# Unread products in the waits of four norms, and ten weight tiles held to the heads of a linear attention

## The chip, the cores and the metric

The kernel runs on one core of one Trainium2 chip. The core has a matrix engine (TensorE, PE), a vector engine (VectorE, DVE), a scalar engine (ScalarE, ACT), a general engine (GpSimd, POOL) and a sync engine (SyncE, SP) that issues most of the transfers; each runs its own instructions in order and waits for the others on semaphores. The metric is the time of one execution on the chip, in microseconds (us). TensorE's clock has two levels, 1.2 and 2.4 GHz; the profile gives the clock that was granted as a share of the higher one (PEclk).

## The reference

One sequence of 512 positions of width 1024 goes through a first block (two kinds of attention, then a mixture of experts looked up by keys) and through two hybrid layers. The change is in the layers. Each mixes three branches under gates, projects, normalises and adds, then does the same with a feed-forward part:

```python
def hybrid_layer(x, ...):
    h = rms_norm_2(x, n_pre_mix)
    proj = h @ w_in
    (u_pool, g_q, g_k, g_v, g_r, g_a1, m_cq, m_ckv, m_kr, gate_logits) = jnp.split(proj, IN_OFFSETS, axis=-1)
    y_a = pool_mixer(u_pool, w_pool, pool_scale) @ w_a
    y_b = gla_mixer(g_q, g_k, g_v, g_r, g_a1, w_gla_a2, b_gla_a, gla_norm) @ w_b
    y_c = mla_mixer(m_cq, m_ckv, m_kr, cos, sin, ...) @ w_c
    gates = jax.nn.sigmoid(gate_logits.astype(jnp.float32)).astype(x.dtype).reshape(b, s, N_BRANCH, d)
    merged = gates[:, :, 0] * y_a + gates[:, :, 1] * y_b + gates[:, :, 2] * y_c
    x = x + rms_norm_2(merged @ w_o, n_post_mix)
    h = rms_norm_2(x, n_pre_ffn)
    gu = h @ w_ffn_gu
    ffn = (jax.nn.silu(gu[..., :D_FF]) * gu[..., D_FF:]) @ w_ffn_down
    return x + rms_norm_2(ffn, n_post_ffn)
```

`gla_mixer` is the linear attention: four heads with keys of 64 and values of 128, in eight chunks of 64 positions. Within a chunk it takes masked scores times values, and between chunks a state that decays:

```python
    cum = jnp.cumsum(heads(log_a, GLA_DK), axis=3)
    att = jnp.where(mask, jnp.einsum('bhntd,bhnsd->bhnts', q_dec, k_inv), 0.0)
    o_intra = jnp.einsum('bhnts,bhnse->bhnte', att, vh)
    kv = jnp.einsum('bhnsd,bhnse->bhnde', k_end, vh)
    ...
    o = (o_intra + o_inter).transpose(0, 2, 3, 1, 4).reshape(b, s, GLA_HEADS, GLA_DV)
    o = o * lax.rsqrt(jnp.mean(o * o, axis=-1, keepdims=True) + EPS)
```

## The kernel before, in words

Activations lie with features on partitions: a tensor of width 1024 is eight tiles of 128 x 512. Every projection goes through `lin`: for each output tile of 128 features and each tile of the input it issues three wide products (`mm3`, L186 to L188), since weights and inputs are split into a high and a low part: high weight by high input, high by low, low by high. A load of weights (`WS.load`, L83 to L102) brings a tile `wr` of 128 x 1024 by SP, ACT casts it to `wh` (L99) and another engine subtracts to get `wl` (L100); there are three buffers of each. A tile serves eight steps, so 24 wide products. Output tiles land in PSUM, are evacuated by a function given to `lin`, and then free their buffer.

In a layer's mix the order is: the input projections, the latent attention, the linear attention `gla`, the gate projection `wgate` (24 output tiles of 24 products), the c projection `wc` and the b projection `wb` (eight output tiles of 12 products each, four weight tiles each), then `wo`. The gate products depend only on the normalised input (`hn`), and the c products only on the latent attention (`yc`), so a scheduler may put them between the small steps of the linear attention. It is a list scheduler that simulates the engines and picks what it thinks is ready, engine by engine; the chip then runs each engine's list in order. `keep_in_program_order` pins an instruction in its engine's order, `issue_after` holds one until a named instruction has been put in. In `load`, the list `hold` says after which instruction the casts of the next weight tiles may go; a held tile's subtraction is on POOL instead of DVE. Before, only the norms fill that list (`self.hold = sq + [self.norm_ins] * 2`, for the three tiles after a norm).

In `gla` the two halves `d` cover heads 0 and 1, then 2 and 3. In each, PE makes the cumulative sums `pc`, `pl` (L718, L719), transposes `tp` (L735) and the chunk states `kv` (L744); ACT copies `kt` (L737); DVE builds the states `st` (L752, L754). For each head PE makes the scores `at` (L762), DVE masks them into `am` (L764), PE makes the output `o` (L768, L774), ACT squares it into `osq` (L776), and PE sums the columns into `pss` (L252). At the end come the norm's broadcast `bc` (L270) and the split into `ybh`, `ybl`.

The gate's evacuation (L607) ends in a store of a tile `sig`. The c evacuation `evc` (L621 to L626) loads that tile into `gc` (two buffers, shared with the gate's `sg`), combines it with PSUM on DVE (L624), adds on POOL (L625) and stores `m` (L626). The b evacuation (L638, L639) has six buffers.

After `wo` and after the ffn's down projection, `post_norm` takes the squares' column sum `pss`, then `rstd_small` (ACT root L260, DVE reciprocal L263), a broadcast `bc` by PE, and per tile DVE's L363 and L364; the next projection starts once ACT has written `hnh` (L316) and DVE `hnl` (L320). There are four such norms: after `wo` and after the ffn in each of two layers.

Of the kernel before, what the change touches and what calls it, by code (L numbers as in the profile page):

```python
# [14 lines left out]
AF = mybir.ActivationFunctionType  # L15
# [5 lines left out]
P = 128  # L21
S = 512
D = 1024
KD = D // P
NT = S // P
# [53 lines left out]
class WS:  # L79
# [7 lines left out]
    def load(self, p):  # L87
        if p not in self.have and p < self.ap.shape[0]:
            nc, wp = self.b.nc, self.b.wp
            raw = wp.tile([P, PW], F32, tag="wr", name="wr", bufs=3)  # L90
            nc.sync.dma_start(raw, self.ap[p])
            hi = wp.tile([P, PW], F32R, tag="wh", name="wh", bufs=3)
            lo = wp.tile([P, PW], F32R, tag="wl", name="wl", bufs=3)
            eng = self.eng
            with ExitStack() as es:
                if self.b.hold:
                    es.enter_context(self.b.tc.issue_after(self.b.hold.pop(0)))
                    eng = nc.gpsimd
                nc.scalar.copy(hi, raw)  # L99
                eng.tensor_tensor(lo, raw, hi.bitcast(F32), OP.subtract)  # L100
            self.have[p] = (hi, lo)
# [14 lines left out]
class Builder:  # L116
# [155 lines left out]
                                  start=True, stop=True)  # L272
        return bc

    def rstd_row(self, parts, dim, sp, hp=None, tok=None, by=1.0):

        p = self.ps(name="pss")
        self.colsum(p, 0, parts, pin=hp is not None)
        r2 = self.rstd_small(p, NT, dim, sp, by)
        bc = self.bcast(r2, 0)  # L280
        if hp is None:
            return bc
        t = hp.tile([P, S], F32, tag="bcs", name="bcs")
        self.nc.any.tensor_copy(t, bc)
        if tok is None:
            return t
        r4 = hp.tile([P, NT], F32, tag=tok, name=tok)
        self.nc.vector.tensor_copy(r4, r2[:, 0:NT])
        return t, r4
# [44 lines left out]
    def post_norm(self, ws, nk, xs, g, side):  # L334

        nc = self.nc
        es = ExitStack()
        sp = self.pool(es, "post", side=side)
        f = sp.tile([P, KD, S], F32, tag="f", name="f")
        parts, sq = [], []  # L340

        def ev(c, p):
            i = self.sq_part(sp, parts, p, c == KD - 1)
            if c == KD - 1:
                sq.append(i.ins)
            if c == KD - 2:
                self.preload(parts[0][:, 0:1])
            if c % 2:
                nc.vector.tensor_scalar(f[:, c], p, g[:, c:c + 1], None, OP.mult)
            else:  # L350
                nc.scalar.activation(f[:, c], p, AF.Copy, scale=g[:, c:c + 1])
        self.lin(ws, nk, KD, xs, ev)
        bc = self.rstd_row(parts, D, sp)
        self.hold = sq + [self.norm_ins] * 2
        old, new = self.xd, self.new_x()

        def get(k):
            self.xd = old
            x = self.x_tile(sp, k, KD if self.final is not None else 5)
            self.xd = new  # L360
            eng = nc.gpsimd if self.final is not None and k in (0, 2, 4) else nc.vector
            pin = self.tc.keep_in_program_order
            pin(nc.vector.tensor_tensor(f[:, k], f[:, k], bc, OP.mult))  # L363
            i = eng.tensor_tensor(x, x, f[:, k], OP.add)  # L364
            if eng is nc.vector:
                pin(i)
            if self.final is not None:
                nc.sync.dma_start(self.final[:, k], x)
            else:
                nc.sync.dma_start(new[k], x)  # L370
            return x
        return get, es
# [124 lines left out]
    def layer_mix(self, l, vb, a, hn, acc, hp, sig_d, ya_d, er):  # L497
        nc = self.nc
        v = self.vecs
        bc = r4 = None  # L500
# [6 lines left out]
        gq = gi.tile([P, 2, S], F32, name="gq")  # L507
        gk = gi.tile([P, 2, S], F32, name="gk")
        gv = gi.tile([P, NT, S], F32, name="gv")
        gr = gi.tile([P, 4, S], F32, name="gr")  # L510
        kr = gi.tile([P, S], F32, name="kr")
# [4 lines left out]
        with ExitStack() as e2:  # L516
            sp = self.pool(e2, "tmpA")
# [48 lines left out]
        with ExitStack() as e2:  # L566
            sp = self.pool(e2, "tmpB")
# [19 lines left out]
        ybh = yp.tile([P, 4, S], F32R, name="ybh")  # L587
        ybl = yp.tile([P, 4, S], F32R, name="ybl")
        gt = self.pool(er, "gates", side="right")
        with ExitStack() as e2:  # L590
            sp = self.pool(e2, "mla")
            for i in range(4):
                o = self.ps("a", name="o")
                self.causal_pair(sp, [([(qT[0:96, h], kT[0:96, h])],
                                       lambda b, h=h: vt[:, b, h * 64:(h + 1) * 64], None)
# [2 lines left out]
        em.close()  # L598
        with ExitStack() as e2:
            gp = self.pool(e2, "gla")  # L600
            self.gla(l, gp, gq, gk, gv, gr, kr[0:32], vb, ybh, ybl)
        eg.close()


        def evg(c, p):
# [6 lines left out]
                nc.vector.scalar_tensor_tensor(t, t, 1.0, y, OP.add, OP.mult)  # L612
            nc.sync.dma_start(sig_d[c], t)
        self.lin_tags = "b"
        self.lin(WS(self, a("wgate")), KD, 24, hn, evg)
        self.lin_tags = "bc"
        m_d = [self.dp.tile([P, S], F32, tag=f"m{i}", name=f"m{i}", bufs=2) for i in range(KD)]
# [75 lines left out]
    def gla(self, l, gp, gq, gk, gv, gr, a1, vb, yh, yl):  # L693
        nc = self.nc
# [13 lines left out]
            nc.vector.scalar_tensor_tensor(la[:, 2 * h:2 * h + 2], z, 0.0, ab, OP.min, OP.subtract)  # L708
        umat, lmat, mask = self.tri[:, 0:P], self.tri[:, P:2 * P], self.tri[:, 2 * P:3 * P]
        oall = gp.tile([P, 4, S], F32, name="oall")  # L710
        pss = self.ps(name="pss")
        for d in range(2):
            ds = slice(d * P, (d + 1) * P)
# [42 lines left out]
            for hh in range(2):  # L756
                h = 2 * d + hh
                r = slice(hh * 64, hh * 64 + 64)
                at = self.ps(shape=[P, NT, P], name="at")
                for b in range(NT):  # L760
                    bs = slice(b * P, (b + 1) * P)
                    nc.tensor.matmul(at[:, b], ki[r, bs], qd[r, bs], start=True, stop=True)  # L762
                am = gp.tile([P, NT, P], F32, tag="am", name="am", bufs=2)
                nc.vector.tensor_tensor(am, at, mask.unsqueeze(1).to_broadcast([P, NT, P]), OP.mult)  # L764
                o = self.ps(name="o")
                for b in range(NT):
                    bs = slice(b * P, (b + 1) * P)
                    nc.tensor.matmul(o[:, bs], gv[:, b, h * P:(h + 1) * P], am[:, b], start=True, stop=False)  # L768
                    for j in range(2):
                        n = 2 * b + j  # L770
                        if n == 0:
                            continue
                        cs = slice(n * 64, n * 64 + 64)
                        nc.tensor.matmul(o[:, cs], st[r, n], qd[r, cs], start=False, stop=j == 1)  # L774
                osq = gp.tile([P, S], F32, tag="osq", name="osq", bufs=2)
                nc.scalar.activation(osq, o, AF.Square)  # L776
                self.colsum(pss, h, [osq])
                nc.any.tensor_copy(oall[:, h], o)
        r2 = self.rstd_small(pss, 16, 128, gp)
        for h in range(4):  # L780
            t = gp.tile([P, S], F32, tag="yt", name="yt", bufs=2)
            bc = self.bcast(r2, h)
            nc.vector.scalar_tensor_tensor(t, oall[:, h], v[:, vb + 36 + h:vb + 37 + h], bc, OP.mult, OP.mult)
            nc.vector.tensor_tensor(t, t, gr[:, h], OP.mult)
            self.split(yh[:, h], yl[:, h], t)

# [1012 lines left out]
```

## Time and profile before

| what | value |
|---|---|
| median of 3 runs | 3681.76 us (3679.64 to 3682.37) |
| the profiled execution | 3670.07 us, its span 3668.3 us |
| mean granted clock of PE | 0.978 |
| busy PE / DVE / ACT / POOL | 3497.4 / 2303.4 / 1397.4 / 1111.2 us |
| busy share of PE | 95% |

The span is one profiled execution on the slowest core; a busy time is the sum over that engine's instructions, and busy PE is not PE at its peak. In the trace the mix of layer 0 ends, with the column sum of its norm, at about 2388 us, the ffn of layer 0 at 2761, the mix of layer 1 at 3279 and the last ffn at about 3651. The linear attention of layer 0 is at about 2204 to 2318.

### The profile page before, as it was taken

What the parts mean: (1) busy time and instruction counts of PE and PEld (TensorE: products, weight loads), DVE (VectorE), ACT (ScalarE), POOL (GpSimd) and SP (SyncE); (2) the same over time, 40 slices, a digit from 0 to 9 for tenths busy, and PEclk for the clock granted to TensorE, in tenths of its full rate; (3) what the DMA queues carried; (4) which work ended last, traced back from release to release, by engine and by line L of the source; (5) the groups of instructions that cost most, each with busy time, mean ns of one, the idle gap of its engine ahead of it and who ended that gap; (6) DMA issues with size and microseconds to landing.
All of it is one profiled execution on the core that took longest, in us unless ns stands there. A gap on an engine that the chain in (4) does not pass through costs nothing.

```text
span 3668.3 us, 46596 instructions
## 1 busy us (share of the span) xinstructions
PE 3497.4 (95%) x17784; PEld 2968.8 (81%) x17784; DVE 2303.4 (63%) x3583; ACT 1397.4 (38%) x2159; POOL 1111.2 (30%) x637
## 2 busy tenths in 40 slices
PE   9979999999999899999999999999999999999998
PEld 7856668998999799888888768878887867778886
DVE  5354454999999699999975544554326363464433
ACT  5534433434665233323333443342223344233221
POOL 1002101666667786666620000231101000131100
PEclk9979999999999999999999999999999999999999
DMA  3212143565888999999952323433333333443332
GB/s 129 96 39 92 55 155 100 185 200 194 295 294 296 328 332 352 351 339 348 340 204 88 131 98 127 158 124 97 109 96 112 115 105 103 158 144 103 96 120 75
DMA packets 229016, 631.25 MB, mean 172 GB/s; under 512 B 22644, under 2 KB 57144, under 8 KB 228792
## 3 DMA queue, kind: packets, MB, share of 16 engines
q1 hardware_dynamic: 191928, 494.04, 39.9%
q0 software_dynamic: 36864, 134.23, 10.2%
q8 instruction: 139, 2.28, 0.3%
q14 instruction: 85, 0.70, 0.1%
HBM read 542.20 MB, written 85.98 MB: 171 GB/s over the span
## 4 chain that ended last, share of the span: by engine, by line
PE 71%; DVE 19%; issue 4%; DMA 2%; ACT 2%; POOL 1%; SPq 1%; ACTq 0%; DVEq 0%; POOLq 0%
PE ps L186 17%; PE ps L188 17%; PE ps L187 17%; PE v L186 3%; PE v L187 3%; PE v L188 3%; DVE og L1561 3%; PE o L415 2%; DVE nr L1411 2%; DVE e L1555 2%; PE s L392 2%; DMA wr<-in_pv 1%; PE tp L409 1%; DVE av L1425 1%; ACT wh L99 1%
## 5 line engine op out<-in xcount | busy, mean ns | idle before, releaser
L99 ACT CAST wh<-wr 128x1024 fp32r<-128x1024 f32 x599 | 626.6, 1050 | 1097.7 <-PE ps L187 741.2
L186 PE MATMUL ps<-hnh,wh 128*128 128x512 f32 (+1 forms) x2616 | 979.7, 378 | 16.2 <-ACT hnh L316 11.3
L188 PE MATMUL ps<-hnh,wl 128*128 128x512 f32 (+1 forms) x2616 | 978.4, 374 | 16.1 <-POOL wl L100 16.1
L187 PE MATMUL ps<-hnl,wh 128*128 128x512 f32 (+1 forms) x2616 | 976.7, 373 | 0.1
L100 POOL TENSOR_TENSOR wl<-wr,wh 128x1024 fp32r<-128x1024 f32 x215 | 562.5, 2618 | 699.7 <-ACT wh L99 592.4
L100 DVE TENSOR_TENSOR wl<-wr,wh 128x1024 fp32r<-128x1024 f32 x384 | 478.3, 1246 | 400.1 <-ACT wh L99 387.2
L186 PEld LDWEIGHTS ps<-hnh,wh 128*128 128x128 f32 x2616 | 498.1, 191 | 85.6 <-ACT hnh L316 12.2
L188 PEld LDWEIGHTS ps<-hnh,wl 128*128 128x128 f32 x2616 | 495.9, 190 | 87.5 <-POOL wl L100 19.6
L187 PEld LDWEIGHTS ps<-hnl,wh 128*128 128x128 f32 x2616 | 496.4, 190 | 67.0 <-DVE hnl L320 2.0
L186 PE MATMUL v<-ah,wh 128*128 128x384 f32 x1024 | 349.8, 342 | 44.9 <-ACT wh L99 44.7
L187 PE MATMUL v<-al,wh 128*128 128x384 f32 x1024 | 345.4, 338 | 0.0
L186 PEld LDWEIGHTS v<-ah,wh 128*128 128x128 f32 x1024 | 193.1, 189 | 57.2 <-ACT wh L99 56.4
L188 PE MATMUL v<-ah,wl 128*128 128x384 f32 x1024 | 228.3, 336 | 0.0
L1411 DVE SCALAR_TENSOR_TENSOR nr<-nr,xt 128x1024 f32<-128x1024 f32 x128 | 210.3, 1658 | 13.5 <-DMA nr<-in_ur,gx 13.5
L1425 DVE SCALAR_TENSOR_TENSOR av<-nr,na,av 128x1024 f32<-128x1024 f32 x127 | 211.4, 1665 | 1.6
L187 PEld LDWEIGHTS v<-al,wh 128*128 128x128 f32 x1024 | 193.3, 189 | 0.0
L675 POOL TENSOR_TENSOR sg<-sg,bcs 128x512 f32<-128x512 f32 x44 | 75.7, 1720 | 374.2 <-ACT sg L674 373.9
L1399 POOL DMA_INDIRECT nr<-in_ur,gx x128 | 176.0, 1375 | 39.7 <-issue 13.1
L188 PEld LDWEIGHTS v<-ah,wl 128*128 128x128 f32 x1024 | 182.9, 188 | 0.9 <-POOL wl L100 0.6
L625 POOL TENSOR_TENSOR gc<-gc,gy 128x512 f32<-128x512 f32 x16 | 24.2, 1513 | 522.6 <-DMA wr<-in_wb 237.8
L223 ACT CAST ah<-at 128x384 fp32r<-128x384 f32 x112 | 57.1, 512 | 328.0 <-DVE at L1334 224.6
L1399 POOL DMA_INDIRECT nr<-in_vr,gx x128 | 161.1, 1259 | 40.3 <-issue 19.0
(490 smaller groups left out, 5534.4 us busy)
## 6 DMA issues: line engine op xcount, KB each, us to landing
wr<-in_pu SPq DMA_DIRECT2D x128, 512.0 KB
wr<-in_pv SPq DMA_DIRECT2D x125, 512.0 KB
wr<-in_wgu SPq DMA_DIRECT2D x88, 512.0 KB
g_d<-gs SPq DMA_DIRECT2D x64, 384.0 KB
gt<-g_d SPq DMA_DIRECT2D x32, 768.0 KB
wr<-in_wgate SPq DMA_DIRECT2D x48, 512.0 KB
wr<-in_wdn SPq DMA_DIRECT2D x44, 512.0 KB
a_d<-ga SPq DMA_DIRECT2D x56, 384.0 KB
```

Of the source, the lines that this page charges most:

```text
L99: nc.scalar.copy(hi, raw)
L100: eng.tensor_tensor(lo, raw, hi.bitcast(F32), OP.subtract)
L186: self.pe(nc.tensor.matmul(out, w[0], x[0], start=start, stop=False))
L187: self.pe(nc.tensor.matmul(out, w[0], x[1], start=False, stop=False))
L188: self.pe(nc.tensor.matmul(out, w[1], x[0], start=False, stop=stop))
L392: nc.tensor.matmul(s[:, 0:n], q[:, t * P:n], k[:, 0:n], start=i == 0, stop=False)
L415: nc.tensor.matmul(o[j * 64:j * 64 + 64, b * P:S], heads[j][1](b), pts[j], start=first and b == 0, stop=last and b == NT - 1)
L675: nc.gpsimd.tensor_tensor(t, t, bc, OP.mult)
L1399: i = nc.gpsimd.indirect_dma_start(out=w[:], out_offset=None, in_=self.a[src], in_offset=bass.IndirectOffsetOnAxis(ap=self.near_i[:, j:j + ...
L1411: nc.vector.scalar_tensor_tensor(u, u, 1.0, xts[group[j]], OP.mult, OP.mult, accum_out=a[:, j:j + 1])
L1425: nc.vector.scalar_tensor_tensor(av, w, a[:, j:j + 1], av, OP.mult, OP.add)
L1561: nc.vector.tensor_tensor(o, e1, two(gT[:, i, tt]), OP.mult)
```

## The change

Two things are added. `keep_awake(n)` issues n products of a 128 x 128 bf16 identity with itself, broadcast to 512 columns, into a PSUM tile `idle` that nothing reads. `rstd_row` takes `warm=(3, 13)` from `post_norm`: three such products between the column sum and the broadcast, thirteen behind the broadcast, all pinned, and the column sum pinned too. That is 64 products in the program.

Secondly `gla` hands out the squares of heads 1, 2 and 3, and the list `hold` gets 28 entries before the gate projection: 18 that hold nothing (the tile is cast whenever it is ready, and subtracted on DVE), then three gate tiles after head 1's square, three after head 2's, and after head 3's the four weight tiles of the c projection.

```diff
-                if self.b.hold:
-                    es.enter_context(self.b.tc.issue_after(self.b.hold.pop(0)))
+                h = self.b.hold.pop(0) if self.b.hold else None
+                if h is not None:
+                    es.enter_context(self.b.tc.issue_after(h))
                     eng = nc.gpsimd
...
+    def keep_awake(self, n):
+
+        p = self.ps(shape=[P, NT, P], name="idle")
+        wide = self.identb.unsqueeze(1).to_broadcast([P, NT, P])
+        for _ in range(n):
+            self.tc.keep_in_program_order(self.nc.tensor.matmul(p, self.identb, wide, start=True, stop=True))
+
-    def rstd_row(self, parts, dim, sp, hp=None, tok=None, by=1.0):
+    def rstd_row(self, parts, dim, sp, hp=None, tok=None, by=1.0, warm=None):
 
         p = self.ps(name="pss")
-        self.colsum(p, 0, parts, pin=hp is not None)
+        self.colsum(p, 0, parts, pin=hp is not None or warm is not None)
+        if warm:
+            self.keep_awake(warm[0])
         r2 = self.rstd_small(p, NT, dim, sp, by)
         bc = self.bcast(r2, 0)
+        if warm:
+            self.keep_awake(warm[1])
...
-        bc = self.rstd_row(parts, D, sp)
+        bc = self.rstd_row(parts, D, sp, warm=(3, 13))
...
-            self.gla(l, gp, gq, gk, gv, gr, kr[0:32], vb, ybh, ybl)
+            late = self.gla(l, gp, gq, gk, gv, gr, kr[0:32], vb, ybh, ybl)
...
+        self.hold = [None] * 18 + [late[i] for i in (0, 0, 0, 1, 1, 1, 2, 2, 2, 2)]
         self.lin(WS(self, a("wgate")), KD, 24, hn, evg)
...
-                nc.scalar.activation(osq, o, AF.Square)
+                late.append(nc.scalar.activation(osq, o, AF.Square).ins)
...
+        return late[1:]
```

PE's list of layer 0 in the first half of the linear attention, before, from the last gate products ahead of head 0's column sum (`ps<-hnh,wh` and its like are gate products):

```order
L187 MATMUL ps<-hnl,wh 128x512
L188 MATMUL ps<-hnh,wl 128x512
L252 MATMUL pss<-ones,osq 128x1 x4
L762 MATMUL at<-qd,ki 128x128 x4
L186 MATMUL ps<-hnh,wh 128x512
L187 MATMUL ps<-hnl,wh 128x512
```

And of the change, from the two gate products behind the transposes to the second head's output (its line numbers are larger by 1 to 14):

```order
L188 MATMUL ps<-hnl,wh 128x512
L189 MATMUL ps<-hnh,wl 128x512
L758 MATMUL kv<-gv,kt 128x256 x7
L776 MATMUL at<-qd,ki 128x128 x4
L782 MATMUL o<-am,gv 128x128
L788 MATMUL o<-qd,st 128x64
...
L788 MATMUL o<-qd,st 128x64 x2
L253 MATMUL pss<-ones,osq 128x1 x4
L776 MATMUL at<-qd,ki 128x128 x4
L782 MATMUL o<-am,gv 128x128
```

Before, 22 gate products stand between head 0's output and its column sum and 23 behind the next scores; from the transposes to head 1's column sum there are 118 in all. Of the change, two are left, and the others stand behind head 1's column sum.

DVE's list at the c projection of layer 0, before (`gc<-gc,ps` is an evacuation of the c projection, `wl<-wr,wh` the subtraction of a weight tile, `am` and `st` belong to heads 2 and 3):

```order
L754 SCALAR_TENSOR_TENSOR st<-st,e_19110,kv 64x128 x2
L624 SCALAR_TENSOR_TENSOR gc<-gc,ps 128x512
L100 TENSOR_TENSOR wl<-wr,wh 128x1024
L754 SCALAR_TENSOR_TENSOR st<-st,e_19110,kv 64x128 x2
L764 TENSOR_TENSOR am<-at,c_tri 128x512
L754 SCALAR_TENSOR_TENSOR st<-st,e_19110,kv 64x128 x2
L624 SCALAR_TENSOR_TENSOR gc<-gc,ps 128x512
L100 TENSOR_TENSOR wl<-wr,wh 128x1024
L624 SCALAR_TENSOR_TENSOR gc<-gc,ps 128x512
L764 TENSOR_TENSOR am<-at,c_tri 128x512
```

And of the change:

```order
L798 TENSOR_TENSOR yt<-yt,gr 128x512
L225 TENSOR_TENSOR ybl<-yt,ybh 128x512 x2
L619 TENSOR_TENSOR sg<-ps,bcs 128x512
L637 SCALAR_TENSOR_TENSOR gc<-gc,ps 128x512 x2
L101 TENSOR_TENSOR wl<-wr,wh 128x1024 x2
L637 SCALAR_TENSOR_TENSOR gc<-gc,ps 128x512 x3
L101 TENSOR_TENSOR wl<-wr,wh 128x1024
L637 SCALAR_TENSOR_TENSOR gc<-gc,ps 128x512
L651 SCALAR_TENSOR_TENSOR gt<-gt,ps 128x512 x2
L228 SCALAR_TENSOR_TENSOR ml<-gt,mh 128x512
```

The evacuations stood among the steps of the linear attention; now they follow it, and the third c evacuation has the subtractions of the first two b tiles ahead of it.

SP's list at the same place, before (`sig` are the stored gate tiles, `m` the stored result of an evacuation, `wr` a load of weights):

```order
L621 DMA gc<-sig_17053 128x512
L626 DMA m_20117<-gc 128x512
L623 DMA gy<-sig_17038 128x512
L621 DMA gc<-sig_17054 128x512
L91 DMA wr<-in_wb 128x1024
L626 DMA m_20118<-gc 128x512
L623 DMA gy<-sig_17039 128x512
L621 DMA gc<-sig_17055 128x512
L626 DMA m_20119<-gc 128x512
```

And of the change:

```order
L91 DMA wr<-in_wb 128x1024
L634 DMA gc<-sig_17054 128x512
L650 DMA gy<-m_20117 128x512
L91 DMA wr<-in_wb 128x1024
L639 DMA m_20118<-gc 128x512
L636 DMA gy<-sig_17039 128x512
L91 DMA wr<-in_wo 128x1024
L634 DMA gc<-sig_17055 128x512
L639 DMA m_20119<-gc 128x512
```

The loads of the last b tiles and the first `wo` tile moved ahead of the c evacuation's third and fourth loads of `gc`.

## Rows read from the trace of the kernel before

**Rows 1.** The page, the chain that ended last by engine.
```profile
PE 71%; DVE 19%; issue 4%; DMA 2%; ACT 2%; POOL 1%; SPq 1%; ACTq 0%; DVEq 0%; POOLq 0%
```

**Rows 2.** Windows: from:to, length, busy (count) per engine, PEclk, DMA share, GB/s.
```profile
2222.00:2237.00 15.00, 15.00 (x76) 11.60 (x75) 9.08 (x19) 3.75 (x5) 0.00 (x0) 1.00 0.30 103
2260.50:2264.00 3.50, 3.50 (x17) 3.38 (x18) 0.00 (x0) 1.18 (x2) 0.00 (x0) 0.53 0.00 0
2301.60:2308.20 6.60, 6.60 (x20) 5.24 (x20) 1.82 (x2) 2.47 (x3) 1.89 (x1) 0.51 0.48 159
222.00:233.00 11.00, 7.97 (x52) 5.46 (x50) 3.67 (x12) 6.26 (x28) 0.00 (x0) 1.00 0.01 1
```

**Rows 3.** Timeline of PE, linear attention: start, length, engine, line, operation [idle before].
```profile
2226.05 0.39 PE L187 MATMUL ps<-hnl,wh 128*128 128x512 f32 x1
2226.28 0.40 PE L188 MATMUL ps<-hnh,wl 128*128 128x512 f32 x1
...
2227.78 1.99 PE L744 MATMUL kv<-gv,kt 64*128 64x256 f32 x14
...
2240.93 0.38 PE L768 MATMUL o<-am,gv 128*128 128x128 f32 x2
...
2244.03 0.66 PE L774 MATMUL o<-qd,st 64*128 64x64 f32 x4
...
2250.74 1.16 PE L762 MATMUL at<-qd,ki 64*128 64x128 f32 x8
...
2261.21 0.79 PE L718 MATMUL pc<-c_tri,la 128*128 128x128 f32 x2
...
2266.59 0.95 PE L252 MATMUL pss<-ones,osq 128*128 128x1 f32 x8
...
2303.62 1.11 PE L774 MATMUL o<-qd,st 64*128 64x64 f32 x4
```

**Rows 4.** Timelines of ACT and DVE, same stretch.
```profile
2222.74 0.59 ACT L737 COPY kt<-tp 128x512 f32<-128x512 f32 x1 [3.01 <-PE tp L735]
...
2229.59 3.37 DVE L754 SCALAR_TENSOR_TENSOR st<-st,e,kv 64x128 f32<-64x128 f32 x9
```

**Rows 5.** Timeline of PE, start of the b projection.
```profile
2319.36 1.20 PE L186 MATMUL ps<-ybh,wh 128*128 128x512 f32 x4 [2.21 <-ACT ybh L223]
```

**Rows 6.** Timelines of DVE, POOL, SP and ACT: c evacuation, weight tiles.
```profile
2295.35 0.69 DVE L624 SCALAR_TENSOR_TENSOR gc<-gc,ps 128x512 f32<-128x512 f32 x1 [3.12 <-DMA gc<-sig]
...
2306.15 1.22 DVE L100 TENSOR_TENSOR wl<-wr,wh 128x1024 fp32r<-128x1024 f32 x1
...
2281.90 1.29 POOL L625 TENSOR_TENSOR gc<-gc,gy 128x512 f32<-128x512 f32 x1 [237.82 <-DMA wr<-in_wb]
...
2387.30 7.42 POOL L100 TENSOR_TENSOR wl<-wr,wh 128x1024 fp32r<-128x1024 f32 x3 [39.15 <-ACT wh L99]
...
2288.26 0.32 SPq L626 DMA_DIRECT2D m<-gc  x1
...
2292.25 0.32 SPq L621 DMA_DIRECT2D gc<-sig  x1
...
2313.20 1.04 ACT L99 CAST wh<-wr 128x1024 fp32r<-128x1024 f32 x1 [0.30 <-DVE rs L263]
```

**Rows 7.** Timelines of PE and DVE: an identity product, norms and their successors.
```profile
183.81 0.39 PE L1138 MATMUL so<-mkb,identb 128*128 128x512 bf16 x1
...
2393.31 2.92 PE L186 MATMUL ps<-hnh,wh 128*128 128x512 f32 x6 [3.46 <-ACT hnh L316]
...
2395.19 0.74 DVE L320 SCALAR_TENSOR_TENSOR hnl<-xk,c_vecs,hnh 128x512 fp32r<-128x512 f32 x1
...
2771.07 0.63 PE L187 MATMUL ps<-hnl,wh 128*128 128x512 f32 x1
2771.50 0.63 PE L188 MATMUL ps<-hnh,wl 128*128 128x512 f32 x1
...
2413.33 0.38 PE L252 MATMUL pss<-ones,sqa 128*128 128x1 f32 x2 [1.27 <-POOL sqa L246]
```

More of the change, by code (lines that the diff above doesn't have):

```diff
@@ L710, in gla @@
         oall = gp.tile([P, 4, S], F32, name="oall")
+        late = []
         pss = self.ps(name="pss")
```

## The prediction

> **What bounds the kernel now.** I read the chain of waits first: TensorE (PE) carries 71% of it [rows 1], so time moves only where PE stands still or runs at its lower clock. Then I cut the linear attention of layer 0 into windows. In a window with gate products between its small steps PE is busy without a gap at granted clock 1.00, yet in two short ones, right behind a block of small products, the clock is 0.53 and 0.51 while PE stays busy [rows 2]. Then PE's timeline: a wide product starts 0.23 us after the one before, so a weight tile (24 of them) is 5.6 us and one output tile of the c or b projection (12) is 2.8 us; the attention's own steps follow with their durations [rows 3]. What they wait for is in the timelines of VectorE (DVE) and ScalarE [rows 4]. The b projection starts after a gap of 2.21 us [rows 5]. Last the path by which the c projection leaves PSUM [rows 6], and the norm after a projection [rows 7]. Layer 1 repeats layer 0, so what follows is for one layer and taken twice, the norms apart.
>
> **First half of the linear attention (heads 0 and 1).** Before, some 118 gate products stand between the transposes and the second column sum; afterwards two. The products are not lost, they come later, but the waits they covered now show. The steps alone take before: kv 1.99, two score blocks of 1.16, an output block 3.76 (2240.93 to 2244.69) and another like it, cumulative sums 3.4 (2261.21 on, at the lower clock), two column sums of 0.95 [rows 3]: 17.2, less 0.1 at each seam, where the next starts before the last ends: 16.5 us.
> Afterwards, from the end of the transposes (t = 0): the copy of kt takes 0.59, so kv runs from 0.6 to 2.6. DVE's state updates start 1.8 behind kv's start (2227.78 to 2229.59) and take 3.37/9 = 0.37 each [rows 3, 4]. The scores need the PSUM buffer that the fourth update frees: 4.0 to 5.1. Their masking stands on DVE behind ten updates, to 6.2, and takes 0.7 (the 128x512 operation of rows 6): the output block can start at 6.9. PE has been busy for 3.6 of 6.9 us.
> At full clock the rest is: output block to 10.7, its square 0.6 and column sum 0.95 to 12.2, scores to 13.4, masking 0.7, output block to 17.9, cumulative sums at half of 3.4 to 19.6, column sum to 20.5. That is 4.0 more than before.
> But a dense mix already fell to 0.53 after one output block [rows 2]; here two and all their waits follow each other with nothing dense between. I let the clock fall before the first output block. At the lower clock four products of that block take 1.11 against 0.66 [rows 3], so the block takes 6.4: to 13.3; square and column sum (0.6 and 1.4) to 15.3, scores (1.9) to 17.2, masking to 17.9, output block to 24.3, cumulative sums 3.4 to 27.7, column sum 1.4 to 29.1. The first gate products behind it start 0.43 apart instead of 0.23 [rows 7]; five of them lose 1.0: 30.1. Against 16.5 this is **+13.6** per layer; bounds +4.0 (clock stays) and +16 (the clock returns later). Against the fall speaks one row: 11 us in which PE was busy for only 8 at clock 1.00 [rows 2].
> The Trainium skill (TensorE: Matmul & The Clock Gate, What's actually happening) says that the clock is set by how busy PE has lately been and that idleness costs half of it. By that rule the fall comes; the trace agrees in two windows and not in the one just named, and no run here shows an attention without cover.
>
> **Second half.** Heads 2 and 3 keep seven and two wide products between their blocks; before, it had more, and still fell to 0.51 for 6.6 us [rows 2]. Two output blocks stand nearly together now: I take **+1.5**, bounds -3.2 (the dip of 6.6 us at half speed goes) and +5.
>
> **Held weight tiles.** The subtraction of a held tile moves to GpSimd, 7.42/3 = 2.5 instead of 1.22 [rows 6]. Behind head 1's square a cast (1.05) and this need 3.6; the cumulative sums and column sum (4.8 at the lower clock) cover them. At full clock 1 us would show. PE then takes 5.6 per tile against 2.5, so nothing else waits. **0**, bounds 0 and +1.5.
>
> **Gap before the b projection.** It goes, since gate and all c products now stand behind the broadcast: **-2.2** [rows 5].
>
> **The c projection without breaks.** Before, its eight output tiles are spread over the second half, one per about 5 us. Now 96 products run on end, 2.8 per output tile, then the b projection's. Tiles 0 to 3 find PSUM free; tile 4 waits for the evacuation of tile 0, and so on. The evacuation has two buffers in turn: DVE 0.69, GpSimd 1.29, store issue to the next load's issue 3.99 (2288.26 to 2292.25; others are as short as 2.6, I take 3.4), and the load, for which DVE waited 3.12 [rows 6] (I take 2.9): 8.3 for two tiles, 4.15 each, against 2.8.
> Two orders make it worse. On DVE the third evacuation stands behind the subtraction of the second b tile. That tile's cast needs the buffer of the third c tile, so PE must have ended output tile 5, at 16.9 after the start: with cast 1.05, subtraction 1.22 and evacuation 0.7 the third is out at 20.0. On SP the load for the fourth stands behind a load of wo that waits for the same subtraction, so it goes out at 19.2, and the fourth is out at 23.3. From these each second one follows 8.3 to 8.4 later: fifth 28.4, sixth 32.6 (SP's order adds the rest).
> PE: output tile 6 starts at 20.0 instead of 16.9 (3.1), tile 7 at 23.4 (0.6), the first b tile at 28.4 (2.2), the second at 32.7 (1.5); later ones find room. **+7.4**, bounds +3 (the order alone, with the shortest store and load) and +13 (the longest, and the clock falling in the gaps).
> The Trainium skill (DMA: Bandwidth & Descriptors, Anatomy of one DMA) puts about 2 us of fixed cost on a transfer, most of it the write receipt. The store and load here measure 3.4 and 2.9. By the page's 2.0 twice, the loop would be 6.0 for two tiles, and what is left is nearly the order alone, about 4, and the sum +28.8; the rows decide.
>
> **The norms.** There are four, each with 3 unread products before its broadcast and 13 behind. The nearest row for one is a bf16 product of that size, 0.39 [rows 7]; at a pitch of 0.23 the 13 take 3.0, inside the wait of 3.46 for the first normalised tile. At the lower clock they take 13 x 0.43 = 5.6, and end 2.1 too late: the bound on the other side. The first L187 behind waits for DVE's hnl (2395.19 + 0.74) whatever the clock [rows 7], so faster products ahead of it give nothing; the gain is the half-speed tail behind it, 0.20 a product (0.43 against 0.23 [rows 3, 7]): three products at the wo norm of layer 0, two at that of layer 1, eight at the ffn norm between the layers. The last norm ends in DVE's work and gains nothing. 2.6 in all, bounds -5 and +6.3. Ten or so more products stand before the column sum of the norm that follows, which fills its wait of 1.27 in layer 0 [rows 7] and its like in layer 1: 2.4. Together **-5.0**.
>
> **Sum.** 2 x (13.6 + 1.5 + 0 - 2.2 + 7.4) - 5.0 = +35.6. On the profiled execution, 3670.07 us (span 3668.3): 3705.7. The median of the runs is 11.7 above that execution, so the forecast is **3717 us**. Its own range is 3704 to 3734.
>
> **The rivals.**
> The clock stays up in the uncovered half, as in the sparse row of rows 2, and the second half is as before: 2 x (4.0 - 2.2 + 7.4) - 5.0 = +13.4, 3695. Against it: two falls in a far denser stretch. Chance 0.2.
> The clock falls, but the evacuation keeps up, because the scheduler's buffers free earlier than I read: 2 x (13.6 + 1.5 - 2.2) - 5.0 = +20.8, 3703. For it: before, the loop held 5 us per tile and PE never waited. Against: the loop was never asked for more. Chance 0.15.
> The unread products run at the lower clock and lie on the path: 2.1 late at three norms, and no gain there: the norms give 6.3 - 2.4 = +3.9 instead of -5.0, so +44.5, 3726. For it: behind the ffn norm the products run 0.43 apart [rows 7]. Chance 0.05.
> Not slower: the clock never falls in the linear attention, because only short interruptions part its blocks. Then the first half costs 4.0, and before's dip of the second half goes (-3.2): 2 x (4.0 - 3.2 - 2.2 + E) - 5.0, with E the evacuation's stalls. With E at its low bound of 3 this is -1.8: 3680; it is no slower from E = 3.9 down. Chance 0.08.
>
> **How the numbers follow.** The forecast's case has 0.52. The range for 8 in 10 is 3690 to 3734: it takes in the first two rivals and most of the third and leaves out the last, the lower edge of the first and the upper ends. About 0.2% (7.4 us) is what a measurement here can tell from no change. Faster by more: 0.06 (the last rival's better half, and 0.02 of the first's edge); within: 0.10; slower: 0.84.
>
> **What would show it.** The windows of the first half at a clock near 0.5 for some 20 us, and PE idle there for several us on DVE's am and ScalarE's kt; waits of PE's c and b products on DVE's gc; no gap on ybh; the norms at clock 1.00 behind the broadcast. The forecast is wrong if the first half shows clock 1.00, or if the c products run through.

## The result, and the profile after

The changed kernel takes 3726.6 us (median of 4 runs, 3725.81 to 3730.15) beside 3680.7 for the kernel before: a ratio of 1.0134, 95% interval 1.0119 to 1.0149, slower by 46 us. The forecast was 3717, with a range of 3690 to 3734. The profiled execution took 3726.86 (span 3725.1).

That is 57 us more than the profiled execution of before, but 7 of them had come before the first layer began (its first product starts at 1877.8 before and at 1884.7 after). That start lies between 1877 and 1888 in all the profiles shown here, and the change does nothing there. So the stages of the layers are compared each by its own length, from one PE instruction to the next of the same name:

| stage, us | before | after |
|---|---|---|
| transposes to the end of heads 0 and 1, layer 0 / 1 | 45.4 / 43.8 | 31.6 / 30.7 |
| from there to the first c product (after), or b product (before), layer 0 | 51.8 | 59.0 |
| all c and b products to `wo`, layer 0 | b alone 22.6 | 53.7 |
| transposes to the column sum of the `wo` norm, layer 0 / 1 | 163.4 / 163.4 | 187.9 / 189.4 |
| that norm, to the first ffn product, layer 0 / 1 | 7.8 / 7.8 | 8.5 / 7.8 |
| ffn, to its down column sum, layer 0 / 1 | 365.4 / 365.3 | 367.0 / 364.5 |
| ffn norm between the layers, and layer 1 to `z` | 336.8 | 335.2 |
| last norm to the end | 18.4 | 17.9 |

The two mixes lost 24.5 and 26.0 us, everything else together gained 0.7. The chain of waits shows no shift, PE still carries it, as in [rows 1]:

```profile
PE 70%; DVE 19%; issue 4%; DMA 3%; ACT 2%; POOL 1%; SPq 0%; DVEq 0%; ACTq 0%; POOLq 0%
```

So the loss is PE time of another kind, and the windows show which. First the uncovered half of the linear attention in layer 0, then its second half, the c run, the wait of the `wo` norm, and a stretch of the ffn behind it (columns as in [rows 2]; the clock stands behind POOL's busy time):

```profile
2236.60:2260.40 23.80, 22.27 (x84) 19.16 (x84) 1.80 (x5) 6.13 (x10) 3.28 (x2) 0.50 0.00 0
2282.90:2304.00 21.10, 20.92 (x87) 16.89 (x86) 1.38 (x2) 7.00 (x9) 6.96 (x3) 0.68 0.27 88
2319.60:2349.20 29.60, 25.62 (x97) 19.35 (x96) 8.10 (x11) 5.86 (x7) 10.81 (x7) 0.88 0.91 322
2421.50:2425.40 3.90, 3.90 (x14) 1.44 (x13) 3.71 (x4) 1.41 (x3) 3.90 (x2) 0.65 0.66 168
2448.00:2455.00 7.00, 7.00 (x21) 5.74 (x21) 2.04 (x3) 1.31 (x2) 0.00 (x0) 0.51 0.22 77
```

Before, the clock was at 0.51 to 0.53 for 3.5 and for 6.6 us [rows 2]. Now it is at 0.50, the lower level of 1.2 GHz, for all 24 us of the first stretch, and at 0.68 over 21 us of the second. PE's timeline in the first half, to be held against [rows 3]:

```profile
2230.33 1.99 PE L758 MATMUL kv<-gv,kt 64*128 64x256 f32 x14 [0.20 <-ACT kt L751]
...
2233.76 1.13 PE L776 MATMUL at<-qd,ki 64*128 64x128 f32 x8 [1.44 <-DVE st L768]
...
2236.66 0.80 PE L782 MATMUL o<-am,gv 128*128 128x128 f32 x2 [1.77 <-DVE am L778]
...
2242.26 1.11 PE L788 MATMUL o<-qd,st 64*128 64x64 f32 x4
...
2244.06 1.87 PE L253 MATMUL pss<-ones,osq 128*128 128x1 f32 x8 [0.69 <-ACT osq L790]
...
2248.71 0.79 PE L782 MATMUL o<-am,gv 128*128 128x128 f32 x2 [0.79 <-DVE am L778]
...
2255.35 0.79 PE L732 MATMUL pc<-c_tri,la 128*128 128x128 f32 x2
```

The waits are those of the walk in the prediction: the scores wait 1.44 for DVE's `st`, the output block 1.77 for `am`, the column sum 0.69 for `osq`. The first output block goes from 2236.66 to 2243.37, 6.7 us against 3.8 in [rows 3]. `kv`, with two gate products just ahead, still ran in 1.99 at full clock.

The c run, from its first product at 2319.65: PE's waits in the window of the c and b products of layer 0, the first two of them in PE's timeline, DVE's evacuations with the subtractions between them, and SP's two loads for the second evacuation (compare [rows 6]):

```profile
PE ps L187 <- DVE gc L637: 5.3, 4, 2.9
```

```profile
2339.57 0.77 PE L187 MATMUL ps<-ych,wh 128*128 128x512 f32 x1 [2.89 <-DVE gc L637]
...
2345.76 0.50 PE L187 MATMUL ps<-ych,wh 128*128 128x512 f32 x1 [0.73 <-DVE gc L637]
```

```profile
2322.66 0.69 DVE L637 SCALAR_TENSOR_TENSOR gc<-gc,ps 128x512 f32<-128x512 f32 x1 [0.58 <-PE ps L189]
...
2332.69 0.69 DVE L637 SCALAR_TENSOR_TENSOR gc<-gc,ps 128x512 f32<-128x512 f32 x1 [9.34 <-DMA gy<-sig]
...
2337.60 1.23 DVE L101 TENSOR_TENSOR wl<-wr,wh 128x1024 fp32r<-128x1024 f32 x1 [3.09 <-ACT wh L100]
2338.75 0.68 DVE L637 SCALAR_TENSOR_TENSOR gc<-gc,ps 128x512 f32<-128x512 f32 x1
...
2345.01 0.69 DVE L637 SCALAR_TENSOR_TENSOR gc<-gc,ps 128x512 f32<-128x512 f32 x1 [5.59 <-DMA gc<-sig]
```

```profile
2327.19 0.50 SPq L634 DMA_DIRECT2D gc<-sig  x1
2327.75 0.54 SPq L636 DMA_DIRECT2D gy<-sig  x1
```

PE's first wait is the one that the prediction walks through. Output tile 6 (the first is 0) starts 19.9 us after the run's start, 2.89 late, and is released by the third evacuation. That one stands at 2338.75 right behind the second subtraction, with no wait of its own; the subtraction waited 3.09 for its cast. The second evacuation was late too, since its loads were issued only at 2327.19 and 2327.75, behind loads that the b projection will want, and DVE waited for them until 2332.69; but no product waited for it. The fourth waited 5.59 for its load. PE waited 5.3 in all, and 3.4 more went because the clock fell in the first wait (0.88 over 29.6 us): 8.7.

The norms behind `wo`, first of layer 0, then of layer 1, as against [rows 7]:

```profile
2421.38 4.39 PE L281 MATMUL idle<-identb 128*128 128x512 bf16 x13
...
2425.41 1.74 PE L187 MATMUL ps<-hnh,wh 128*128 128x512 f32 x6
...
3339.09 2.97 PE L281 MATMUL idle<-identb 128*128 128x512 bf16 x13
...
3342.73 1.66 PE L187 MATMUL ps<-hnh,wh 128*128 128x512 f32 x6 [0.67 <-ACT hnh L328]
```

In layer 0 the thirteen products took 4.39 instead of 3.0: the clock had fallen all the same (0.65), and the first ffn product came 0.7 late. In layer 1 they took 2.97 and cost nothing.

### The profile page after: what moved, and what is told of

It reads as the page before. It is cut to its first block, busy times and chain, and to the rows that moved or that the text cites. A ratio compares the mean times of both kernels' runs of the same rounds, so it can differ in the third digit from the quotient of the medians.

```text
span 3725.1 us, 46710 instructions
## 1 busy us (share of the span) xinstructions
PE 3549.6 (95%) x17848; PEld 3002.4 (81%) x17848; DVE 2287.3 (61%) x3563; ACT 1402.2 (38%) x2163; POOL 1158.6 (31%) x657
## 4 chain that ended last, share of the span: by engine, by line
PE 70%; DVE 19%; issue 4%; DMA 3%; ACT 2%; POOL 1%; SPq 0%; DVEq 0%; ACTq 0%; POOLq 0%
PE ps L187 17%; PE ps L189 17%; PE ps L188 16%; PE v L187 3%; PE v L188 3%; PE v L189 3%; DVE og L1576 3%; DVE nr L1426 2%; PE o L427 2%; DVE e L1570 2%; DMA wr<-in_pv 2%; PE s L404 2%; PE tp L421 1%; ACT wh L100 1%; DVE e L1572 1%
## 5 line engine op out<-in xcount | busy, mean ns | idle before, releaser
L101 POOL TENSOR_TENSOR wl<-wr,wh 128x1024 fp32r<-128x1024 f32 x235 | 612.3, 2608 | 1214.7 <-ACT wh L100 1099.4
L101 DVE TENSOR_TENSOR wl<-wr,wh 128x1024 fp32r<-128x1024 f32 x364 | 454.2, 1248 | 396.9 <-ACT wh L100 391.1
L187 PE MATMUL v<-ah,wh 128*128 128x384 f32 x1024 | 350.9, 343 | 43.9 <-ACT wh L100 43.8
L187 PE MATMUL ps<-hh,wh 128*128 128x512 f32 x352 | 136.9, 389 | 0.0
```

The lines of the kernel that those rows point to most:

```text
L187: self.pe(nc.tensor.matmul(out, w[0], x[0], start=start, stop=False))
```

## The experiments

Each ran beside the kernel before on the same chip; ratios are to it. Runs 1, 2, 3 and 5 were one set (median of before 3676.5), runs 4, 6, 7 and 8 another on a second chip (3677.4), so between the sets, and with the change (3680.7), the ratios are what compares. The stage lengths are from one profile of each run.

**1. Only the unread products.**

```diff
-        self.hold = [None] * 18 + [late[i] for i in (0, 0, 0, 1, 1, 1, 2, 2, 2, 2)]
```

> Only the unread products at the four norms; no hold (the gate and c products stand in the linear attention as before). Theory: of the 46 us that the change lost, the norms are nearly none; they move the time by -4 to +2 us against before (3680.7), since in two of the three norms the 13 products ran at granted clock 0.65 and delayed the next projection by 0.6 us, and only the stretch behind them gained. Rival (the price in the prediction): -5 us, about 3676. Second rival: they cost what is missing in the forecast (46 against 36), so +10.

3669.56 us, ratio 0.9975 (0.9963 to 0.9986): faster than before, by 6.9 us between the medians. In its profile the layers, from their first product to the end, take 5.5 us less than before: ffn 0 gained 2.1 and ffn 1 2.0 (the tail at half clock, and the wait ahead of the next norm's column sum), the stretch behind the norm between the layers 2.9, a b projection without a dip 1.5; that norm itself lost 2.3. The 1.5 lie where this edit does nothing. My theory (-4 to +2) underrated it; the prediction's -5.0 was close. What took the norm's 2.3 us:

```profile
2767.79 1.44 PE L281 MATMUL idle<-identb 128*128 128x512 bf16 x3
...
2769.02 1.91 PE L271 MATMUL bc<-c_ident,rs 128*128 128x128 f32 x8
...
2770.73 3.03 PE L281 MATMUL idle<-identb 128*128 128x512 bf16 x13
...
2775.32 1.66 PE L187 MATMUL ps<-hnh,wh 128*128 128x512 f32 x6 [1.56 <-ACT hnh L328]
```

The three products ahead of the broadcast ran at half speed (1.44 against 0.81 in other norms), so did most of the broadcast (1.91 against 1.13), and everything behind came later. The thirteen then ended 1.56 before they were needed.

**2. Only the hold.**

```diff
-        bc = self.rstd_row(parts, D, sp, warm=(3, 13))
+        bc = self.rstd_row(parts, D, sp)
```

> Only the hold list; no unread products. Theory: all of the loss is here, 3724 to 3731 us, +24 to +26 in each layer's mix as in the profile of the change. Rival: the pinned column sums and unread products shift the lists of the next stages and carry 10 us of it, so 3717.

3728.71 us, ratio 1.0135 (1.0118 to 1.0152). The whole loss is in the hold. By the ratios (1.0135 here, 1.0134 for the change) a gain of the unread products beside the hold can't be told from none; by the layers of the two profiles it is 3.6 us.

**3. Only the c tiles held.**

```diff
-        self.hold = [None] * 18 + [late[i] for i in (0, 0, 0, 1, 1, 1, 2, 2, 2, 2)]
+        self.hold = [None] * 24 + [late[2]] * 4
```
(and no unread products)

> No unread products; only the four weight tiles of the c projection are held to head 3's square, the gate tiles are free. Theory: the first half of the linear attention is as before (clock near 1, no waits), the second half now runs without cover and costs what the first half cost in the change (13 us), the c run keeps its waits on the evacuation (8.7), the gap of 2.2 goes: +17 to +20 per layer, 3715 to 3721. Rival A (the evacuation loop is harmless when the c tiles start late): +11 per layer, 3703. Rival B (cover matters only where the gate products stood): +7 per layer, 3695.

3707.41 us, ratio 1.0078 (1.0061 to 1.0095), +31 by the medians; the stages from the second transposes to the `wo` column sum lose 15.8 in layer 0 and 13.2 in layer 1, 1 to 4 short of the theory's low end and above both rivals' +11 and +7. The term that fell short is the uncovered half. Without its wide products it takes 26.2 us in both layers, where it took 16.8 before: 9.4 more and not 13 (before, 3.2 of it had already gone to the dip of [rows 2]). The first half is as before (43.8 us in both layers, like layer 1 before). The second half now shows what the first showed in the change:

```profile
2282.55 0.67 PE L758 MATMUL kv<-gv,kt 64*128 64x256 f32 x2 [1.44 <-DVE st L768]
...
2286.21 0.79 PE L782 MATMUL o<-am,gv 128*128 128x128 f32 x2 [1.78 <-DVE am L778]
...
2302.92 1.87 PE L253 MATMUL pss<-ones,osq 128*128 128x1 f32 x8 [0.69 <-ACT osq L790]
```

The same waits of 1.4, 1.8 and 0.7, and behind the first of them the lower clock. So the cover is what counts, not which products give it.

**4. Only the gate tiles held.**

```diff
+        self.hold = [None] * 18 + [late[i] for i in (0, 0, 0, 1, 1, 1)]
```
(and no unread products)

> No unread products; the six gate tiles held, the four c tiles free (subtracted on DVE as soon as their buffers are free). Theory: the c tiles come behind the held gate tiles in the same three buffers, so holding them adds nothing: as the hold alone, 3726 to 3730. Rival: the held c tiles' subtractions on GpSimd stand in the way of the evacuation's additions there; without the hold the c run's waits halve, 3719 to 3722.

3721.27 us, ratio 1.0127 (1.0111 to 1.0142): the median is in the rival's range, 7 us below the hold with the c tiles, but the intervals of the two ratios overlap. PE's order in the mix is the same in both, and the c run's waits on `gc` did not halve: 4.0 and 4.7 us in the two layers, against 6.0 and 7.2. The mix is 2 us shorter in each layer than in run 2, and the rest lies in small pieces, 1.5 in each ffn among them. Holding the c tiles on top of the gate tiles costs little; whether it costs anything stays open.

**5. Four buffers for the evacuation of the c projection.**

```diff
+        ce = self.pool(er, "cev", side="right")
-            t = gt.tile([P, S], F32, tag="sg", name="gc", bufs=2)
+            t = ce.tile([P, S], F32, tag="gc", name="gc", bufs=4)
-            y = gt.tile([P, S], F32, tag="sy", name="gy", bufs=2)
+            y = ce.tile([P, S], F32, tag="gcy", name="gy", bufs=4)
```

> The change, with four buffers instead of two for the c projection's evacuation (its two tiles get a pool of their own, no longer shared with the gate's). Theory: the c and b products wait because the evacuation goes round two buffers; with four they run through, 45 us for 192 products instead of 53.7: 8 us less per layer than the change, 3710 to 3713. Rival A (the order on DVE and SP is the limit, the evacuation stands behind weight tiles that wait for the same products): the buffers give at most 3 per layer, 3721 to 3726. Rival B (the transfers are late because the queues are full, clock and bandwidth): no gain, 3726.

3700.05 us, ratio 1.0059 (1.0042 to 1.0076): 26.5 us less than the change by the medians, more than the 14 to 17 expected. What was to be shown is in two views, PE's waits in the same stretch, and the windows of the c and of the b products:

```profile
PE ps L187 <- DVE gt L652: 0.8, 1, 0.8
```

```profile
2310.00:2334.00 24.00, 24.00 (x104) 19.31 (x103) 9.59 (x12) 6.41 (x7) 12.04 (x7) 1.00 0.96 348
2334.00:2358.00 24.00, 23.22 (x100) 18.41 (x99) 17.60 (x18) 7.43 (x10) 14.79 (x9) 1.00 0.91 326
```

No wait on `gc` is left, and the clock stays at 1.00. From the broadcast to the `wo` column sum the mix is 7.7 and 7.3 us shorter per layer than in the change, as the theory had it. But the buffers moved DVE's order with them: the first four evacuations now stand ahead of the first subtraction.

```profile
2321.67 0.69 DVE L638 SCALAR_TENSOR_TENSOR gc<-gc,ps 128x512 f32<-128x512 f32 x1 [2.12 <-PE ps L189]
2322.57 2.25 DVE L101 TENSOR_TENSOR wl<-wr,wh 128x1024 fp32r<-128x1024 f32 x1 [0.20 <-ACT wh L100]
```

So the run shows that the evacuation makes the waits, and not how much of them is the loop over two buffers and how much the order. The other 10 us by the profiles lie elsewhere: 4.4 of them in the ffn of layer 0, where the change had its stretch at half clock, and 3.8 ahead of the c run of layer 1, where PE's list is another.

**6. The change, and unread products in the waits of the first half.**

```diff
+W_AT, W_O, W_S = (6, 0), (7, 3), (3, 0)
...
+                if d == 0:
+                    self.keep_awake(W_AT[hh])
                 at = self.ps(shape=[P, NT, P], name="at")
...
+                if d == 0:
+                    self.keep_awake(W_O[hh])
                 am = gp.tile([P, NT, P], F32, tag="am", name="am", bufs=2)
...
+                if d == 0:
+                    self.keep_awake(W_S[hh])
                 self.colsum(pss, h, [osq], pin=d == 0)
```
(and the block's own products pinned; 19 unread ones a layer, not the 22 of the expectation)

> The change, and in the first half of the linear attention unread products in the waits: 6 before the first scores, 7 and 3 before the output blocks, 3 before the first column sum, 3 before the second scores' block at most (22 a layer, 5 us at full clock, as long as the waits). The order of all else is that of the change. Theory: of the 13 us that the first half lost per layer, 4 are waits and 9 the lower clock, and the clock falls because PE stands still between the blocks; with the waits filled it stays up and the first half is 8 to 9 us shorter: 3708 to 3711. Rival A: the small products themselves pull the clock down, filled waits or not; the unread products run at half speed, outlast the waits and cost 2 to 4 per layer: 3730 to 3735. Rival B: the clock stays up for a part only, 3715 to 3722.

3726.23 us, ratio 1.0138 (1.0121 to 1.0155): not to be told from the change.

```profile
2230.10:2241.00 10.90, 10.90 (x64) 7.44 (x65) 3.72 (x10) 1.18 (x2) 0.00 (x0) 0.98 0.01 2
2241.00:2253.00 12.00, 12.00 (x47) 10.22 (x46) 0.54 (x2) 4.58 (x7) 2.91 (x2) 0.50 0.00 0
```

```profile
2230.09 1.47 PE L284 MATMUL idle<-identb 128*128 128x512 bf16 x6 [1.35 <-DVE st L773]
...
2232.57 1.68 PE L284 MATMUL idle<-identb 128*128 128x512 bf16 x7
...
2234.09 0.38 PE L793 MATMUL o<-am,gv 128*128 128x128 f32 x2
...
2237.20 0.66 PE L801 MATMUL o<-qd,st 64*128 64x64 f32 x4
...
2240.61 1.44 PE L284 MATMUL idle<-identb 128*128 128x512 bf16 x3
...
2247.27 1.11 PE L801 MATMUL o<-qd,st 64*128 64x64 f32 x4
```

Through the first output block the clock now stayed at 0.98, with small products in 0.66 where the change has 1.11, and the block took 3.8. Ahead of the second it fell all the same, although PE was busy without a gap from 2230.09 on. The half is 3.5 us shorter in layer 0 (26.4 instead of 29.9 to its last column sum) and 1.2 in layer 1. What follows takes this back: in layer 0 PE's list now has 33 gate products ahead of the second transposes instead of 22 and so fewer behind them, and from the end of the first half to the first c product 144 gate products and the second half take 63.8 us instead of 59.0. Of the theory one part fell: PE need not stand still for the clock to fall. Here it fell among small products with the waits filled. The first fill did not work as meant either: its PSUM buffer came free only with DVE's fourth update, so it waited the 1.35 it was to cover. Rival A fits in this, but not in its price, and no run shows what dense products inside the blocks themselves would do.

**7. Eight unread products behind the broadcast instead of thirteen, no hold.**

```diff
-        bc = self.rstd_row(parts, D, sp, warm=(3, 13))
+        bc = self.rstd_row(parts, D, sp, warm=(3, 8))
```

> Only the unread products, 3 before the broadcast and 8 behind it instead of 13. Theory: what the products give is the clock behind the norm and not their number; 8 end before the first normalised tile even at half speed, so the norms that lost 0.6 to 2.3 us lose less: 1 to 3 us faster than with 13 (3669.6), 3667 to 3669. Rival: with 8 the clock falls in the rest of the wait, and the gain is lost: 3674 to 3677.

3670.28 us, ratio 0.9986 (0.9977 to 0.9995); with thirteen 3669.56. The two can't be told apart. By the stages it gained 8.0 against 5.5, but 1.6 of the difference lie in the first half of layer 0, where nothing differs. The norm between the layers lost the same 2.3, and in both profiles the clock had fallen ahead of the broadcast. With thirteen, the same norm lost 0.6 in the change and in run 6, and nothing in runs 5 and 8: whether the clock falls in that norm changes from one profile to the next, so this run does not show what the number behind the broadcast is worth.

**8. The unread products, and only the last two c tiles held.**

```diff
+        self.hold = [None] * 26 + [late[2]] * 2
```

> The unread products (3, 13) and only the last two c tiles held to head 3's square; gate tiles and the first two c tiles are free. Theory: 22 c products now stand behind the broadcast, so the gap of 2.2 us before the b projection goes; head 3 loses 17 products of cover and pays about 1 to 2 us for it: 0 to 1 us per layer better than with the unread products alone (3669.6), 3668 to 3670. Rival: head 3's output block runs at half speed and the evacuation has four c tiles on end, +4 per layer: 3677.

3672.94 us, ratio 0.9990 (0.9981 to 0.9999). The gap before the b projection is gone; its first product stands behind a c product without a wait:

```profile
2320.28 3.73 PE L271 MATMUL bc<-c_ident,rs 128*128 128x128 f32 x32
...
2329.00 0.40 PE L187 MATMUL ps<-ybh,wh 128*128 128x512 f32 x1
```

Yet from the second transposes to the `wo` column sum layer 0 takes 1.3 us more than before and layer 1 0.2 more: what the 22 products cover behind the broadcast, they no longer cover at head 3, where PE now stands still for 0.9. Of all versions the first, the unread products alone, has the lowest median, though its interval overlaps those of runs 7 and 8.

## Why the prediction was right, by its steps

**The first half** was forecast at +13.6 a layer, 1.0 of it for the first gate products behind it. The steps without the gate products took 17.8 before (45.4 less 118 products of 0.234) and 31.1 after: +13.3 in layer 0, and by the same sum +14.1 in layer 1, against the 12.6 that remain. The walk held at each wait (1.44, 1.77, 0.69), and the clock fell before the first output block, as chosen. The reason given was two blocks and all their waits with nothing dense between. The waits are not needed for it: in run 6 the clock fell with them filled, and the two dips of [rows 2], which the prediction counted for a fall by idleness, show PE busy for all of 3.50 and 6.60 us.

**The second half** was mis-sized: +1.5 forecast, with a bound of +5. In layer 0, from the end of the first half to the first c product, PE had 144 wide products (33.7 us) and 25.3 of other things; before, to the first b product, 124 (29.0) and 22.8, the gap of 2.2 among them. So the gap went, and the rest is +4.7 (the 1.0 for the first gate products belongs here). The clock accounts for it: 21 us at 0.68 lose 6.7 where before 6.6 us at 0.51 lost 3.2, and the first gate products behind the uncovered half ran at half speed longer than the five I allowed, at 0.74 until 2267, which loses 1.7:

```profile
2260.40:2267.00 6.60, 6.60 (x24) 5.29 (x24) 5.33 (x3) 0.44 (x1) 4.18 (x2) 0.74 0.67 215
```

I counted the cover of that half as nearly unchanged, since gate products stand in it; but 22 of them stand behind the last output block and 7 and 2 between the blocks. In layer 1 the same sum gives +7.5, outside the bounds: its list has 32 gate products ahead of the second transposes instead of 22, and from these to the last column sum PE stands still for 1.9 us and the clock is 0.74 (0.2 us and 0.82 in layer 0).

**The gap** of 2.2 before the b projection went, as forecast.

**The c projection** was +7.4, and measured +8.7 in layer 0 and +8.3 in layer 1 (53.7 and 53.3 us for 192 products of 45.0). The first wait came as walked through: tile 6 started at 19.9 and 2.89 late, for 20.0 and 3.1. Then the terms part. The clock fell in that wait, tile 6 took 5.5 us instead of 2.8, and behind it PE waited 0.73, 0.42 and 1.26 where 0.6, 2.2 and 1.5 were forecast. So the waits came to 5.3 instead of 7.4, and the clock, which stood in the upper bound alone, cost 3.4: that the sum came so near is in part luck. A load was priced at 2.9, and the two for the second evacuation took about five us. That the evacuation is the cause is shown by run 5, which took away the waits and 7 to 8 us a layer, by buffers and order together.

**The norms** were -5.0. Between the profiles of before and of the change everything outside the mixes came to -0.7: the clock fell in two of the three norms that count in spite of the products (0.7 and 0.6 late), and a new stretch at half clock opened behind the column sum in the middle of the ffn of layer 0 (0.51 from 2448 to 2455, about 3 us lost). But single profiles don't settle so small a sum. Outside the mixes, from the first product of the layers on, the four profiles without unread products (before, runs 2, 3, 4) take 1463.7 to 1468.2 us, 1465.6 in the mean, and the six with them 1458.2 to 1464.5, 1460.6 in the mean: 5.0 less, with the hold as without it. So the size was right. The parts were not: the prediction gives each norm a fixed gain, and each gains or loses up to 3 us by whether the clock falls there in that profile.

**The sum**: 2 x (13.3 + 4.7 - 2.2 + 8.7) - 0.7 = 48.3 from layer 0's terms, against 49.9 between the profiles' layers and 46 between the medians. The forecast's 35.6 lacked 1.4 of the first half, 4.4 of the second, 2.6 of the c run and, by these two profiles, 4.3 of the norms. Of the rivals, the one with the evacuation that keeps up (+20.8) was run as the four buffers: +23.6 against the median of all before runs shared with it. The rival with the clock up did not come, nor did the one on the other side. The one with the unread products on the path came in part, 0.7 and 0.6 late at two norms instead of 2.1.

## What to carry to other kernels

Wide products that can be issued at any time were worth most here between the small steps of a dependent chain: they hide the waits, and with them there the clock stayed up, which here weighed more than the waits (8.4 of the 13.3 us of the first half, beside 4.9). Before work is held for a late gap, price what it covers where it stands: here a gap of 2.2 us a layer was closed and 27 us a layer were opened. When work that was spread is bunched, check the evacuation behind it: an evacuation over two buffers, by the prediction's estimate 8.3 us for two tiles, made PE wait nowhere at one tile per 5 us and did at one per 2.8.

## What the runs showed that I had not expected

In the sixth run the clock fell among small products with PE busy throughout (0.50 over 12 us, with PE busy for all 12 and for the 10.9 ahead of them). And a short pause does not decide by its length: at the column sum in the middle of the ffn of layer 0, the clock was at 1.00 before, behind a wait of 1.27, and fell for 7 us in the change, behind a wait of 0.64. Gains of 2 to 4 us from such places should be read from several profiles.
